# Hybrid S5 + mLSTM trunk on one core: S5 outputs by position, copies moved between engines, buffers and staging rearranged

## The chip, the cores and the metric

One Trainium2 chip, one core. The metric is the device time in microseconds of one execution. Its engines are TensorE (PE in the profile, its weight loads PEld), VectorE (DVE), ScalarE (ACT), GpSimd (POOL) and SyncE (SP, which issues the DMA transfers here).

## What is computed

One layer of a streaming encoder on x of 2048 positions x 1024 channels, then a final RMSNorm:

```python
h = rmsnorm(x, g);  p = h @ W_in
u, q_raw, k_raw, v, o_raw, i_raw, f_raw = split(p)
y_ssm = s5_mixer(u)     # 32 groups x 16 channels, one 64-dim complex state per group
                        # y = Re(C x) + D u ; z = gelu(y); z * sigmoid(z @ w_glu + b); rmsnorm
y_ml = mlstm_mixer(...) # 4 heads x 128; width-4 conv + SiLU on q, k; gates; rmsnorm per head
x = x + concat(y_ssm, y_ml) @ W_out
x = x + relu(rmsnorm(x) @ W1)^2 @ W2     # 1024 -> 4096 -> 1024
return rmsnorm(x)
```

## The kernel before

**Number format.** Large products run in fp16 as three matmuls: high x high, high x low, low x high (mm3, lines 155 to 161, where L159, L160 and L161 are the three). The high part is made by a scaled copy, the low part by a scaled subtraction. Weights are scaled and split when loaded (load_w, from L127): the usual path is one ACT copy with a scale (L140) and one DVE scalar_tensor_tensor (L141) per slice of 128 rows. With E=G it is, for eight slices, a DVE scaling of each (L134), an ACT copy for each two (L136) and a POOL subtraction for each two (L137). S5's small matmuls are in float32.

**Stages of the trace.** 0 to 150 us: input norm, the u projection, S5 tables. 150 to 690: the mixers, 16 blocks b (4 heads x 4 blocks of 512 positions). 690 to 740: the turn to the output projection. 740 to 912: output projection. 912 to 1500: FFN phase 0 (first half of the positions). 1500 to 2110: phase 1. To 2181: the last FFN outputs and the final norm.

**Mixer.** Block b makes q and k for the next block (proj_qk: 24 matmuls into a PSUM tile pq; then ACT copies pq to xc behind three halo columns, L236, and starts the convolution, L237; POOL copies the halo in, L239, and the next one out, L244; three DVE steps, L247; tanh; L250), v and the output gate (proj_vo), scores (mix_scores), the running state (mix_state) and the output (mix_out). mix_out multiplies the gate by the numerator, sums squares on ACT (L889), makes the norm factor in v4 with small DVE and POOL operations (L892 to L896) and scales og by v4 on POOL (L897). mix_store(b), called in block b+1, transposes og on PE (L904), splits it (L908, L909) and stores it to DRAM (L910).

**S5.** Sixteen units u of two groups run in blocks 0 to 10. s5_const(u) makes tables that depend on parameters only: inm and xt (POOL through helper line L603, DVE through L606), ge (three POOL copies, L630 to L632), the Toeplitz matrix in PSUM tile pgg (PE, L636 and L637, from ge and xt), its four shifted copies into m0 (ACT, L643) and the D term added to m0 by two DVE instructions (L645); then inT (L648, L650), the rotation table rh (POOL and DVE, one buffer) and four transfers from rh to rt (L670, on SP's queue; rt has two buffers). s5_state(u) transposes u (L686), projects it to states (L691), rotates (L694 to L698), scans (L700) and rotates back into sv (L702 to L708). s5_out(u) makes py: for each of two halves and two groups one matmul of m0 (L718) and one of xt (L719). Then GELU on ACT and DVE (L722 to L726) into uz. The GLU steps (glu_a, L764, reads uz by position within 8) follow from block 11 on. PSUM pool psa (tag "ax") has two buffers, shared by pgg, pit, put, pw and py.

**FFN.** A Strassen-like scheme with seven products. In a loop of phase 0, each step issues twelve matmuls of 512 columns (L1351 to L1353). The second operands, for phase 1, are made beside it by a generator hprep1 of 60 steps: loads of b, the norm (L1137), differences (L1146), a split on ACT and POOL (L1081, L1082), a store to DRAM. From loop step HP1 = 46 on, every second step advances it by one.

**Order.** Each engine takes its queue in order. The order is made by a planner at build time, which simulates a timeline and places each instruction when its simulated inputs are ready, so work of later units may stand far ahead of its place in the program. Tiles of one tag are handed out in program order.

**Memory.** Pools are stacked from two sides. The first two hop tiles (operands of the FFN products and before them of the output projection, pool hopa) lie on the right side behind r3, over addresses that the late mixer tiles used. The store of the last mixer block and the load of the first hop go through SP's queue (L910, L1292).

Of the kernel before, what the change touches and what calls it, by code (L numbers as in the profile page):

```python
# [9 lines left out]
F32 = mybir.dt.float32  # L10
# [7 lines left out]
P = 128  # L18
# [11 lines left out]
SLACK = 6  # L30
HP1 = 46
HB = 256
# [15 lines left out]
def trunk(  # L48
# [176 lines left out]
    def proj_qk(b, w):  # L225
# [12 lines left out]
        if t > 0:  # L238
            G.tensor_copy(xc[:, 0:3], halo[w])  # L239
        else:  # L240
            G.memset(xc[:, 0:3], 0.0)
        if t < NTB - 1:
            hl = smal.tile([P, 3], F32, name=f"hl{nm}{w}", tag=f"hl{w}", bufs=2)
            G.tensor_copy(hl, xc[:, TB:TB + 3])  # L244
            halo[w] = hl
# [32 lines left out]
    G.memset(Jm, 1.0)  # L278
    G.affine_select(out=Jm.rearrange("p (q i) -> p q i", i=8), in_=Jm.rearrange("p (q i) -> p q i", i=8), pattern=[[-1, 16], [16, 8]], compare_op=ALU.is_equal, fill=0.0, base=-112, channel_multiplier=1)
    pwr = cp.tile([P, 9, NG], F32, name="pwr")  # L280
# [314 lines left out]
    def s5_const(u):  # L595
# [20 lines left out]
        def bk(a, n):  # L616
            return a.unsqueeze(2).to_broadcast([P, 2, n, 16])
# [11 lines left out]
        gev = ge.rearrange("p g e (j q) -> p g e j q", q=16)  # L629
        G.tensor_copy(gev[:, :, 0, 0::2, :], bk(eb, 4))  # L630
        G.tensor_copy(gev[:, :, 0, 1::2, :], bk(inm[:, :, 1], 4))
        G.tensor_copy(gev[:, :, 1, 1::2, :], bk(eb, 4))  # L632
        pg = psa.tile([P, 2, P], F32, name=f"pgg{u}", tag="ax")
        for g in range(2):
            xf = xt[:, g].rearrange("p k q -> p (k q)")
            T.matmul(pg[:, g, 0:16], ge[:, g, 1, :], xf[:, 0:16], start=True, stop=True)  # L636
            T.matmul(pg[:, g, 16:128], ge[:, g, 0, :], xf[:, 0:112], start=True, stop=True)  # L637
        m0 = m02[u % 2]
        m0v = m0.rearrange("p g (q i) -> p g i q", i=8)
        pgv = pg.rearrange("p g (i q) -> p g i q", q=16)  # L640
        for a in range(4):
            o = 6 - 2 * a
            S.copy(m0v[32 * a:32 * a + 32, :, o:8, :], pgv[32 * a:32 * a + 32, :, 0:8 - o, :])  # L643
        for g in range(2):
            V.scalar_tensor_tensor(out=m0[:, g, :], in0=Jm, scalar=ct[:, O_D + g0 + g:O_D + g0 + g + 1], in1=m0[:, g, :], op0=ALU.mult, op1=ALU.add)  # L645
        pit = psa.tile([P, 2, P], F32, name=f"pit{u}", tag="ax")
# [4 lines left out]

        rh = st("rh", (2, 16, 16))
        tc_, td_ = (st(t, (2, 16, 16))[:, 0] for t in ("t1", "t2"))
# [57 lines left out]
    def s5_out(u):  # L711
        g0 = 2 * u
        xt, m0 = s5u.pop(u)[0:2]
        us, sv = s5s.pop(u)
        py = psa.tile([P, 2, 2, P], F32, name=f"py{u}", tag="ax")
        for h in range(2):
            for g in range(2):
                T.matmul(py[:, h, g, :], us[:, g, h, :], m0[:, g, :], start=True, stop=False)  # L718
                T.matmul(py[:, h, g, :], sv[:, g, h * P:(h + 1) * P], xt[:, g, 1:9, :].rearrange("p k q -> p q k"), start=False, stop=True)  # L719

        y2 = s5.tile([P, 2, 2, P], F32, name=f"y2{u}", tag="y2")
        S.activation(out=y2, in_=py, func=AF.Square)  # L722
        V.scalar_tensor_tensor(out=y2, in0=y2, scalar=1.0 / 0.044715, in1=py, op0=ALU.add, op1=ALU.mult)
        S.activation(out=y2, in_=y2, func=AF.Tanh, scale=GC * 0.044715)
        for h in range(2):
            V.scalar_tensor_tensor(out=uz[h][:, g0:g0 + 2, :], in0=y2[:, h], scalar=1.0, in1=py[:, h], op0=ALU.add, op1=ALU.mult)  # L726
        if u % 4 == 3:
            m = u // 4
            for h in range(2):
                V.tensor_reduce(out=zmx[:, h, m:m + 1], in_=uz[h][:, 8 * m:8 * m + 8, :].rearrange("p g n -> p (g n)"), axis=AX.X, op=ALU.max, apply_absolute_value=True)  # L730
# [28 lines left out]
    def glu_a(n):  # L759
# [3 lines left out]
        zc = gp.tile([P, 512], F32, name=f"zc{n}", tag="zc", bufs=3)  # L763
        V.tensor_scalar(out=zc.rearrange("p (g q) -> p g q", q=16), in0=uz[h].rearrange("p g (q i) -> p i g q", i=8)[:, i], scalar1=zs, scalar2=None, op0=ALU.mult)  # L764
        pz = psl.tile([P, 4, P], F32, name=f"pz{n}", tag="ml")
# [104 lines left out]
    def mix_out(b):  # L870
# [25 lines left out]
        V.scalar_tensor_tensor(out=v4, in0=v4, scalar=0.5, in1=rc, op0=ALU.mult, op1=ALU.mult)  # L896
        G.tensor_tensor(out=og, in0=og, in1=v4.unsqueeze(2).to_broadcast([P, 4, P]), op=ALU.mult)  # L897

# [16 lines left out]
    def load_wo(i, slot=0, wp=None, tag=None):  # L915
        wo[i], m = load_w(wout[i], KD, 256, O_GOUT, f"out{i}", slot, wp, tag, E=G)
        r_w[i] = descale(m, 2.0 ** -24, f"out{i}", tag="dsw")
# [62 lines left out]

    accxp = ctx.enter_context(pool("accx", side="right"))
    r3 = ctx.enter_context(pool("r3", side="right"))
    hopa = ctx.enter_context(pool("hopa", side="right"))
    hopp = [hopa, hopa] + [None] * 5
# [572 lines left out]
    for i in range(N + LAG):  # L1557
        if i < N:
            next(f1)
        if i >= HP1 and (i - HP1) % 2 == 0:  # L1560
            next(hp1, None)
# [96 lines left out]
```

## Time and profile before

| | |
|---|---|
| Median of 3 runs | 2182.2 us (2182.05 to 2182.97) |
| Profiled execution, own time | 2182.95 us |
| Its span | 2180.9 us |
| Mean granted TensorE clock | 0.982 |
| PE busy | 2042.0 us, 94% |
| DVE busy | 1711.0 us, 78% |
| ACT busy | 1062.5 us, 49% |
| POOL busy | 1150.6 us, 53% |

The profiled execution is one program run recorded by the hardware profiler. Busy time is the time in which an engine had an instruction running; shares are of the span. Matmuls overlap at their ends, so a busy PE is an upper reading of its work. "a <- b" after a group names what released it from its idle time: the instruction or transfer that came last. The chain of waits follows the work that ended last back through its releasers, and gives each line's share.

### The profile page before, as it was taken

To read this page: it belongs to the slowest core of one execution; us is meant where nothing else is said; L and a number is where in the kernel's file an instruction comes from. 1 tells how busy PE (TensorE), PEld (TensorE's weight loads), DVE (VectorE), ACT (ScalarE), POOL (GpSimd) and SP (SyncE) were. 2 spreads that over 40 slices of the span, in tenths; PEclk is the share of its full clock that TensorE was granted. 3 is DMA by queue.
4 is the path that set the end of the run, shared out by engine and by line. 5 is a ranking of instruction groups with operands and counts; after the bars stand their busy time and mean duration, and the time that the engine had idled before them with its cause. 6 is when DMAs were issued, how large, how long until landed. Compare 5 with 4: busy or idle time off the path is not lost.

```text
span 2180.9 us, 30020 instructions
## 1 busy us (share of the span) xinstructions
PE 2042.0 (94%) x11205; PEld 1162.8 (53%) x11205; DVE 1711.0 (78%) x2850; ACT 1062.5 (49%) x1902; POOL 1150.6 (53%) x1112
## 2 busy tenths in 40 slices
PE   6999998899999699999899999999999999999996
PEld 4986777677676344444344443444444444444445
DVE  7878888877867645769898999887888887677776
ACT  5425555555544322355454554555565555554543
POOL 2135656564323302466656766756685667565635
PEclk9999999999999899999999999999999999999998
DMA  4211111212103212311222222215342232111112
GB/s 167 68 52 54 54 40 35 73 35 64 59 20 115 108 39 77 112 49 44 92 87 69 101 92 77 79 53 199 99 153 97 97 116 81 55 67 50 39 39 78
DMA packets 55732, 168.18 MB, mean 77 GB/s; under 512 B 7905, under 2 KB 21409, under 8 KB 43041
## 3 DMA queue, kind: packets, MB, share of 16 engines
q1 hardware_dynamic: 55584, 166.26, 22.7%
q8 instruction: 88, 1.44, 0.3%
q14 instruction: 60, 0.48, 0.1%
HBM read 129.44 MB, written 28.41 MB: 72 GB/s over the span
## 4 chain that ended last, share of the span: by engine, by line
PE 48%; DVE 26%; POOL 7%; DMA 5%; issue 5%; ACT 4%; SPq 1%; POOLq 0%; DVEq 0%; ACTq 0%
DVE w2o L1227 3%; PE gx L1351 3%; PE gx L1352 3%; PE gx L1353 3%; PE fx L1351 3%; PE fx L1352 3%; PE fx L1353 3%; DMA r<-in_w_dram 3%; DVE x L1447 2%; PE po L159 2%; PE po L160 2%; PE po L161 2%; DVE y L247 2%; PE fv L1351 1%; PE fv L1352 1%
## 5 line engine op out<-in xcount | busy, mean ns | idle before, releaser
L1226 ACT ACTIVATE w2o<-r,fs_b 128x768 f16<-128x768 f32 (+1 forms) x128 | 105.4, 824 | 135.3 <-POOL r L1284 60.2
L1352 PEld LDWEIGHTS <-w2o 128*128 128x128 f16 x952 | 93.3, 98 | 131.8 <-issue 36.5
L1380 ACT ACTIVATE e<-e 128x512 f32<-128x512 f32 x96 | 60.3, 628 | 203.7 <-DVE e L1416 89.2
L1227 DVE SCALAR_TENSOR_TENSOR w2o<-r,fs_b,w2o 128x768 f16<-128x768 f32 (+1 forms) x128 | 134.7, 1053 | 25.1 <-ACT w2o L1226 24.3
L1353 PEld LDWEIGHTS <-w2o 128*128 128x128 f16 x952 | 93.1, 98 | 103.9 <-DVE w2o L1227 3.2
L1351 PEld LDWEIGHTS <-w2o 128*128 128x128 f16 x952 | 93.5, 98 | 103.0 <-ACT w2o L1226 3.1
L161 PE MATMUL pv<-w_vo,xn 128*128 128x256 f16 x512 | 141.1, 276 | 0.4 <-DVE xn L445 0.3
L159 PE MATMUL pv<-w_vo,xn 128*128 128x256 f16 x512 | 141.2, 276 | 0.0
L160 PE MATMUL pv<-w_vo,xn 128*128 128x256 f16 x512 | 141.2, 276 | 0.0
L1447 DVE SCALAR_TENSOR_TENSOR x2b<-gx,dd,x2b 128x512 f32<-128x512 f32 x112 | 82.7, 744 | 53.1 <-PE gx L1353 53.0
L1284 POOL TENSOR_TENSOR r<-r,s 128x256 f32<-128x256 f32 x64 | 63.9, 999 | 111.8 <-DVE w2o L1227 111.8
L1447 DVE SCALAR_TENSOR_TENSOR x<-gx,dd,x 128x512 f32<-128x512 f32 x128 | 94.2, 741 | 10.7 <-PE gx L1353 10.5
L1240 POOL TENSOR_TENSOR s<-r 128x512 f32<-128x512 f32 x32 | 54.1, 1690 | 85.4 <-issue 59.9
L159 PE MATMUL pq<-xn,w_qk 128*128 128x512 f16 x256 | 99.0, 387 | 0.0
L160 PE MATMUL pq<-xn,w_qk 128*128 128x512 f16 x256 | 98.7, 386 | 0.0
L161 PE MATMUL pq<-xn,w_qk 128*128 128x512 f16 x256 | 98.7, 385 | 0.0
L1351 PE MATMUL fx<-hop,wB 128*128 128x512 f16 x256 | 97.0, 379 | 0.7 <-ACT e L1409 0.7
L1352 PE MATMUL fx<-hop,wB 128*128 128x512 f16 x256 | 97.0, 379 | 0.0
L1353 PE MATMUL fx<-hop,wB 128*128 128x512 f16 x256 | 97.0, 379 | 0.0
L159 PEld LDWEIGHTS <-xn 128*128 128x128 f16 x768 | 87.8, 114 | 9.8 <-ACT xn L444 0.5
L160 PEld LDWEIGHTS <-xn 128*128 128x128 f16 x768 | 87.8, 114 | 9.4 <-issue 0.5
L161 PEld LDWEIGHTS <-xn 128*128 128x128 f16 x768 | 87.5, 114 | 8.9 <-DVE xn L445 1.8
(1326 smaller groups left out, 6940.0 us busy)
## 6 DMA issues: line engine op xcount, KB each, us to landing
r<-in_w_dram SPq DMA_DIRECT2D x64, 1024.0 KB, 4.9
xt<-in_xN_dram SPq DMA_DIRECT2D x16, 512.0 KB, 4.3
rt<-rh SPq DMA_DIRECT2D x64, 128.0 KB, 2.3
hopd<-ho SPq DMA_DIRECT2D x28, 256.0 KB, 2.6
hop<-hopd SPq DMA_DIRECT2D x7, 1024.0 KB, 4.7
st_vo<-in_wvo_dram SPq DMA_DIRECT2D x4, 1024.0 KB, 5.2
st_qk<-in_wqk_dram SPq DMA_DIRECT2D x4, 1024.0 KB, 5.2
bcm<-negM_d SPq DMA_DIRECT2D x16, 256.0 KB, 3.1
```

Source lines behind the costliest of these rows:

```text
L159: T.matmul(out, wh, xh, start=(i == 0), stop=False)
L160: T.matmul(out, wh, xl, start=False, stop=False)
L161: T.matmul(out, wl, xh, start=False, stop=(i == n - 1))
L1226: S.activation(out=hi, in_=src, func=AF.Copy, scale=sg)
L1227: V.scalar_tensor_tensor(out=lo, in0=src, scalar=sg, in1=hi, op0=ALU.mult, op1=ALU.subtract)
L1240: G.tensor_tensor(out=s12[:, 0], in0=raw[:, 2], in1=raw[:, 3], op=ALU.add)
L1284: G.tensor_tensor(out=r[:, 1], in0=r[:, 1], in1=s12[:, 1], op=ALU.subtract)
L1351: T.matmul(out, wh, xh, start=(first and i == 0), stop=False, skip_group_check=True)
L1352: T.matmul(out, wh, xl, start=False, stop=False, skip_group_check=True)
L1353: T.matmul(out, wl, xh, start=False, stop=(last and i == n - 1), skip_group_check=True)
L1380: S.activation(out=x, in_=x if src is None else src, func=AF.Relu, scale=scale)
L1447: V.scalar_tensor_tensor(out=acc[:, j, c, :], in0=bk[b], scalar=dd, in1=acc[:, j, c, :], op0=ALU.mult, op1=ALU.add)
```

## The change

In the S5 units the py columns go by position (i, then q) instead of (q, then i): m0, the D pattern Jm, the moving operand of L719 and the read in glu_a follow. The D term is added in PSUM, on the 32 columns where it lies, ahead of the four copies; a small table Jd is made for that at the start with four POOL copies. The ge copies, the halo copies and the og norm move from POOL to ACT (the norm as four activations with a scale per partition); the next halo is read from PSUM. rh has two buffers. load_wo takes load_w's usual path. Pool hopa is opened before r3. hprep1 starts at step 38 and is advanced in three of eight steps.

```diff
--- before.py
+++ after.py
@@ -28,7 +28,7 @@
 NFB = DFF // 256
 XF = 128.0
 SLACK = 6
-HP1 = 46
+HP1 = 38
 HB = 256
 NHD = 23
 EPS = 1e-6
@@ -236,12 +236,12 @@
         S.activation(out=xc[:, 3:], in_=pq, func=AF.Copy)
         S.activation(out=y, in_=pq, func=AF.Identity, scale=wc[:, 3:4], bias=cb[:, w:w + 1])
         if t > 0:
-            G.tensor_copy(xc[:, 0:3], halo[w])
+            S.copy(xc[:, 0:3], halo[w])
         else:
             G.memset(xc[:, 0:3], 0.0)
         if t < NTB - 1:
             hl = smal.tile([P, 3], F32, name=f"hl{nm}{w}", tag=f"hl{w}", bufs=2)
-            G.tensor_copy(hl, xc[:, TB:TB + 3])
+            S.copy(hl, pq[:, TB - 3:TB])
             halo[w] = hl
         for j in range(1, 4):
             V.scalar_tensor_tensor(out=y, in0=xc[:, 3 - j:3 - j + TB], scalar=wc[:, 3 - j:4 - j], in1=y, op0=ALU.mult, op1=ALU.add)
@@ -276,7 +276,11 @@
     G.memset(sgn[64:128], -1.0)
     Jm = cp.tile([P, P], F32, name="Jm")
     G.memset(Jm, 1.0)
-    G.affine_select(out=Jm.rearrange("p (q i) -> p q i", i=8), in_=Jm.rearrange("p (q i) -> p q i", i=8), pattern=[[-1, 16], [16, 8]], compare_op=ALU.is_equal, fill=0.0, base=-112, channel_multiplier=1)
+    G.affine_select(out=Jm.rearrange("p (i q) -> p i q", i=8), in_=Jm.rearrange("p (i q) -> p i q", i=8), pattern=[[16, 8], [-1, 16]], compare_op=ALU.is_equal, fill=0.0, base=-112, channel_multiplier=1)
+
+    Jd = cp.tile([P, 32], F32, name="Jd")
+    for a_ in range(4):
+        G.tensor_copy(Jd[32 * a_:32 * a_ + 32, :], Jm[32 * a_:32 * a_ + 32, (6 - 2 * a_) * 16:(8 - 2 * a_) * 16])
     pwr = cp.tile([P, 9, NG], F32, name="pwr")
     pwi = cp.tile([P, 9, NG], F32, name="pwi")
     Lc = cp.tile([P, 16, 16], F32, name="Lc")
@@ -627,29 +631,29 @@
 
         ge = ge2[u % 2]
         gev = ge.rearrange("p g e (j q) -> p g e j q", q=16)
-        G.tensor_copy(gev[:, :, 0, 0::2, :], bk(eb, 4))
-        G.tensor_copy(gev[:, :, 0, 1::2, :], bk(inm[:, :, 1], 4))
-        G.tensor_copy(gev[:, :, 1, 1::2, :], bk(eb, 4))
+        S.copy(gev[:, :, 0, 0::2, :], bk(eb, 4))
+        S.copy(gev[:, :, 0, 1::2, :], bk(inm[:, :, 1], 4))
+        S.copy(gev[:, :, 1, 1::2, :], bk(eb, 4))
         pg = psa.tile([P, 2, P], F32, name=f"pgg{u}", tag="ax")
         for g in range(2):
             xf = xt[:, g].rearrange("p k q -> p (k q)")
             T.matmul(pg[:, g, 0:16], ge[:, g, 1, :], xf[:, 0:16], start=True, stop=True)
             T.matmul(pg[:, g, 16:128], ge[:, g, 0, :], xf[:, 0:112], start=True, stop=True)
+        for g in range(2):
+            V.scalar_tensor_tensor(out=pg[:, g, 0:32], in0=Jd, scalar=ct[:, O_D + g0 + g:O_D + g0 + g + 1], in1=pg[:, g, 0:32], op0=ALU.mult, op1=ALU.add)
         m0 = m02[u % 2]
-        m0v = m0.rearrange("p g (q i) -> p g i q", i=8)
+        m0v = m0.rearrange("p g (i q) -> p g i q", i=8)
         pgv = pg.rearrange("p g (i q) -> p g i q", q=16)
         for a in range(4):
             o = 6 - 2 * a
             S.copy(m0v[32 * a:32 * a + 32, :, o:8, :], pgv[32 * a:32 * a + 32, :, 0:8 - o, :])
-        for g in range(2):
-            V.scalar_tensor_tensor(out=m0[:, g, :], in0=Jm, scalar=ct[:, O_D + g0 + g:O_D + g0 + g + 1], in1=m0[:, g, :], op0=ALU.mult, op1=ALU.add)
         pit = psa.tile([P, 2, P], F32, name=f"pit{u}", tag="ax")
         for g in range(2):
             T.transpose(pit[:, g, :], inm[:, g].rearrange("p k q -> p (k q)"), ident)
         inT = st("inT", (2, P))
         S.copy(inT, pit)
 
-        rh = st("rh", (2, 16, 16))
+        rh = st("rh", (2, 16, 16), 2)
         tc_, td_ = (st(t, (2, 16, 16))[:, 0] for t in ("t1", "t2"))
 
         def hk(a):
@@ -716,7 +720,7 @@
         for h in range(2):
             for g in range(2):
                 T.matmul(py[:, h, g, :], us[:, g, h, :], m0[:, g, :], start=True, stop=False)
-                T.matmul(py[:, h, g, :], sv[:, g, h * P:(h + 1) * P], xt[:, g, 1:9, :].rearrange("p k q -> p q k"), start=False, stop=True)
+                T.matmul(py[:, h, g, :], sv[:, g, h * P:(h + 1) * P], xt[:, g, 1:9, :].rearrange("p k q -> p (k q)"), start=False, stop=True)
 
         y2 = s5.tile([P, 2, 2, P], F32, name=f"y2{u}", tag="y2")
         S.activation(out=y2, in_=py, func=AF.Square)
@@ -761,7 +765,7 @@
         gp = gl["p"]
         zs = gl["z"][1][:, h:h + 1]
         zc = gp.tile([P, 512], F32, name=f"zc{n}", tag="zc", bufs=3)
-        V.tensor_scalar(out=zc.rearrange("p (g q) -> p g q", q=16), in0=uz[h].rearrange("p g (q i) -> p i g q", i=8)[:, i], scalar1=zs, scalar2=None, op0=ALU.mult)
+        V.tensor_scalar(out=zc.rearrange("p (g q) -> p g q", q=16), in0=uz[h].rearrange("p g (i q) -> p i g q", i=8)[:, i], scalar1=zs, scalar2=None, op0=ALU.mult)
         pz = psl.tile([P, 4, P], F32, name=f"pz{n}", tag="ml")
         for m in range(4):
             T.transpose(pz[:, m, :], zc[:, m * P:(m + 1) * P], ident)
@@ -894,7 +898,8 @@
         V.tensor_scalar(out=v4, in0=v4, scalar1=0.25 / P, scalar2=EPS, op0=ALU.mult, op1=ALU.add)
         G.tensor_tensor(out=v4, in0=v4, in1=nhalf, op=ALU.pow)
         V.scalar_tensor_tensor(out=v4, in0=v4, scalar=0.5, in1=rc, op0=ALU.mult, op1=ALU.mult)
-        G.tensor_tensor(out=og, in0=og, in1=v4.unsqueeze(2).to_broadcast([P, 4, P]), op=ALU.mult)
+        for c in range(4):
+            S.activation(out=og[:, c, :], in_=og[:, c, :], func=AF.Copy, scale=v4[:, c:c + 1])
 
     def mix_store(b):
         h, t = b // NTB, b % NTB
@@ -913,7 +918,7 @@
     wo, r_w = [None] * 4, [None] * 4
 
     def load_wo(i, slot=0, wp=None, tag=None):
-        wo[i], m = load_w(wout[i], KD, 256, O_GOUT, f"out{i}", slot, wp, tag, E=G)
+        wo[i], m = load_w(wout[i], KD, 256, O_GOUT, f"out{i}", slot, wp, tag)
         r_w[i] = descale(m, 2.0 ** -24, f"out{i}", tag="dsw")
 
     mix_load(0)
@@ -979,8 +984,8 @@
 
 
     accxp = ctx.enter_context(pool("accx", side="right"))
+    hopa = ctx.enter_context(pool("hopa", side="right"))
     r3 = ctx.enter_context(pool("r3", side="right"))
-    hopa = ctx.enter_context(pool("hopa", side="right"))
     hopp = [hopa, hopa] + [None] * 5
     accx = [None] * 4
 
@@ -1557,7 +1562,7 @@
     for i in range(N + LAG):
         if i < N:
             next(f1)
-        if i >= HP1 and (i - HP1) % 2 == 0:
+        if i >= HP1 and (i - HP1) * 3 % 8 < 3:
             next(hp1, None)
         if i == 16:
             w2_scale(0, 0)
```

## Rows read from the trace of the kernel before

**Rows 1.** Windows: us, busy us (instructions) of PE, PEld, DVE, ACT, POOL; clock, DMA.

```profile
150.00:565.00 415.00, 385.11 (x2658) 299.45 (x2657) 336.19 (x663) 219.78 (x535) 233.75 (x292) 0.97 0.18 50
...
690.00:740.00 50.00, 26.15 (x157) 17.35 (x155) 36.28 (x88) 16.86 (x39) 17.71 (x16) 0.83 0.53 195
...
1000.00:1415.00 415.00, 389.43 (x1785) 176.60 (x1784) 374.02 (x511) 208.40 (x310) 275.45 (x228) 0.99 0.24 81
1415.00:1500.00 85.00, 84.99 (x398) 39.05 (x396) 69.17 (x102) 45.31 (x65) 47.60 (x43) 1.00 0.25 92
```

**Rows 2.** Chain of waits, 150 to 565 us: its sum by line.

```profile
by line: DVE y L247 8.9%; DMA rt<-rh 4.9%; DVE t L700 4.8%; issue 4.3%; ACT m L643 3.6%; SPq L670 3.2%; PE pq L159 2.9%; PE pq L160 2.8%; DVE w_vo L141 2.7%; PE pq L161 2.6%; DVE t L698 2.3%; DVE m L645 2.3%; DVE rh L606 2.0%; DVE t L704 1.
```

**Rows 3.** Groups of PE by shape, 150 to 565 us: busy us, mean ns, idle before.

```profile
L719 PE MATMUL py<-xt,sv 128*128 128x128 f32 x128 | 38.6, 391 | 6.1 <-POOL sv L708 4.7 <-POOL xc L241 1.3
L718 PE MATMUL py<-m,us 128*128 128x128 f32 x128 | 26.3, 287 | 1.7 <-ACT m L643 1.7
...
L904 PE MATMUL pT<-ident,og 128*128 128x128 f32 x44 | 7.1, 284 | 6.7 <-POOL og L897 5.0 <-POOL sv L707 1.7
```

**Rows 4.** Timeline of PE at 452 us: start us, us, engine, line.

```profile
452.49 0.39 PE L718 MATMUL py<-m,us 128*128 128x128 f32 x2
452.71 0.60 PE L719 MATMUL py<-xt,sv 128*128 128x128 f32 x2
453.13 0.40 PE L718 MATMUL py<-m,us 128*128 128x128 f32 x2
```

**Rows 5.** Groups of DVE by shape, 150 to 565 us.

```profile
L645 DVE SCALAR_TENSOR_TENSOR m<-Jm,ct,m 128x128 f32<-128x128 f32 x32 | 16.7, 561 | 7.3 <-ACT m L643 7.3
...
L865 DVE SCALAR_TENSOR_TENSOR C<-C,gbc,pst 128x129 f32<-128x129 f32 x39 | 13.4, 342 | 8.5 <-PE pst L860 8.3
...
L606 DVE TENSOR_TENSOR rh<-Hs,Lc 128x256 f32<-128x256 f32 x15 | 12.3, 822 | 14.6 <-DMA rt<-rh 14.6
...
L885 DVE TENSOR_TENSOR rc<-pn,gcol 128x2 f32<-128x2 f32 x22 | 3.3, 149 | 0.2 <-PE pn L883 0.2
```

**Rows 6.** Line 645 alone: duration ns minimum/median/maximum.

```profile
L645 DVE SCALAR_TENSOR_TENSOR m<-Jm,ct,m x32: 321/350/1357, 164.6 to 524.4; 128x128 f32<-128x128 f32 x32
```

**Rows 7.** Groups of POOL by shape, 150 to 565 us.

```profile
L603 POOL TENSOR_TENSOR rh<-Hc,Lc 128x256 f32<-128x256 f32 x15 | 16.5, 1098 | 22.1 <-DMA rt<-rh 20.3 <-DVE og L887 1.7
...
L897 POOL TENSOR_TENSOR og<-og,v 128x512 f32<-128x512 f32 x11 | 14.2, 1289 | 4.8 <-DVE v L896 4.7
...
L632 POOL COPY ge<-bcA 128x128 f32<-128x128 f32 x15 | 7.7, 515 | 34.1 <-PE pgg L636 34.1
```

**Rows 8.** Window 150 to 565 us, instructions on tile ge alone.

```profile
150.00:565.00 415.00, 18.60 (x128) 17.57 (x128) 21.32 (x45) 0.97 0.18 50
```

**Rows 9.** Groups of ACT by shape, 150 to 565 us.

```profile
L829 ACT ACTIVATE sc<-bcm,gbc 128x128 f32<-128x128 f32 x44 | 14.2, 389 | 0.1
...
L889 ACT ACTIVATE kw<-og 128x128 f32<-128x128 f32 x44 | 13.1, 300 | 6.9 <-DVE og L887 6.8
...
L643 ACT COPY m<-pgg 32x256 f32<-32x256 f32 x16 | 9.9, 620 | 0.2
...
L650 ACT COPY inT<-pit 128x256 f32<-128x256 f32 x16 | 5.9, 369 | 1.0 <-PE pit L648 0.7
```

**Rows 10.** Timeline of PE, 709 to 733 us.

```profile
731.41 0.77 PE L98 MATMUL pmx_out<-ident,m_out 128*128 128x128 f32 x2 [13.52 <-DVE m_out L110]
```

**Rows 11.** Timeline of SP's issues, 716 to 733 us.

```profile
722.05 0.33 SPq L910 DMA_DIRECT2D ml_d<-mo  x1
722.47 0.38 SPq L129 DMA_DIRECT2D st_out<-in_wout_dram  x1
```

**Rows 12.** Timeline of POOL, 715 to 733 us.

```profile
716.92 2.45 POOL L137 TENSOR_TENSOR w_out<-st_out,w_out 128x512 f16<-128x512 f32 x2
```

**Rows 13.** Groups of DVE by shape, 1000 to 1415 us.

```profile
L1137 DVE SCALAR_TENSOR_TENSOR b<-b,ct,rsh 128x512 f32<-128x512 f32 x16 | 19.0, 1200 | 0.0
...
L1146 DVE TENSOR_TENSOR b<-b,b 128x512 f32<-128x512 f32 x12 | 15.5, 1291 | 3.2 <-POOL ho L1082 3.2
```

## Prediction, made before the result was known

> **What bounds the kernel now.** I read the page first, then a table by stage. In the mixer, 150 to 565 us, PE is busy 385.11 of 415.00 us, DVE 336.19 (81%), POOL 233.75 (56%) and ACT 219.78 (53%) [rows 1]: PE comes close to full, so the stage is worth attacking in two ways only, fewer PE microseconds or fewer PE stalls. The idle 29.9 us is the least that stalls cost here, as ends of matmuls are modelled. The other stages that the change touches are the turn from mixer to FFN (690 to 740, PE 26.15 of 50) and FFN phase 0 (1000 to 1415, PE 389.43 of 415, DVE 374.02); from 1415 to 1500 PE is full at 84.99 of 85 with DVE at 69.17 [rows 1].
>
> Then the chain of waits for the mixer: it is not on one engine. DVE y L247 has 8.9%, the transfer rt<-rh 4.9% and SP's issue of it (L670) 3.2%, the m copies (L643, ACT) 3.6%, the D term (L645, DVE) 2.3% [rows 2]. So an S5 unit's table, Toeplitz block and scan run beside the projections, and PE stalls where the planner's order expects them sooner than they come. Last, the groups by engine and the PE timeline, for the durations below.
>
> **Outputs by position (L719).** The second matmul of a py pair reads xt with q before k, a stride of 16 elements; it takes 391 ns, where L718 with the same shape takes 287 [rows 3]. In the timeline a pair is 452.49, 452.71, 453.13: the strided one holds PE 0.42 us, the other 0.22 [rows 4]. The new order reads xt contiguously. If L719 falls to 0.22 to 0.24 us, a pair gains 0.19, and 16 units x 4 pairs x 0.19 = **12 us**, all of it PE time and PE is the fullest engine. Were the stride not the reason (L718 differs from it in weights only), it is 0. I take 12: same shape, type and engine, and the moving operand's order is what differs. The other end stays in the range.
>
> The same layout makes the target of the four m copies contiguous. The largest takes 620 ns for 32x256, the inT copy 369 for 128x256 from the same kind of PSUM tile, contiguous on both sides [rows 9]: 16 x 0.25 = 4 us of ACT for this size alone, in a chain of which L643 holds 3.6% [rows 2]. The zc read in the GLU gets runs of 16 in place of a stride; I cost it at nothing, since at worst it stays as it is.
>
> **D term in PSUM (L645).** Removed: 32 x 561 ns = 18 us (16.7 us in the window [rows 5]) on SBUF 128x128. Added: 32 instructions of 128x32 with one PSUM input. No such row exists. The nearest from PSUM are L865, 128x129 at 342 ns, and L885, 128x2 at 149 [rows 5]: in proportion 149 + 30/127 x 193 = 195 ns, so 32 x 0.195 = 6.2 and DVE loses 10 to 11 us. With L885 as one end and L865 as the other the new term is 4.8 to 10.9 us. In a stage where DVE is 81% busy and PE 93% little of that is path: 2.3% of 415 us is 9.5 us of chain [rows 2], of which a part goes and the next chain takes over. I take **2**, between 0 and 6.
>
> The old row's minimum is 321 ns, its median 350 and its maximum 1357 [rows 6]. So the mean of 561 comes from some instructions that were held up, and the unhindered saving is only 0.35 - 0.20 = 0.15 us each, 5 us in all. [...]
>
> **Copies and norm off GpSimd.** POOL loses the ge copies (21.32 us, x45 [rows 8]), the og norm (11 x 1289 ns = 14.2 us) [rows 7] and the 3-column halo copies. ACT gains 48 ge copies at some 0.30 (L889, 128x128, 300 ns), 4 scaled copies per block at 0.389 (L829 with a pointer, 44 here = 17.1 us), and 32 halo copies of at most 0.30 each [rows 9]: 14.4 + 17.1 + 9.6 = 41, less 4 = **37 us**, so ACT goes from 53% to 62%. POOL falls by over 35 us, to 48%. What is bought: PE waited 5.0 us for og at L904 and 4.7 us for POOL's sv at L719 [rows 3]. The norm's latency falls little (four times 0.389 = 1.56 against 1.29 us), but it need no longer queue behind POOL's 1.3 to 1.6 us tables. I take 60% of these 9.7 us, **6** (sv's own tables stay on POOL), and charge ACT's fuller queue **2** (py and pT wait for its evacuations): net 4. Bounds: 10 gained to 34 lost (last rival).
>
> **Two table buffers (rh).** DVE stood 14.6 us [rows 5] and POOL 20.3 us [rows 7] before the next rh, waiting for the transfer out of the only one. With two, unit u+1's table no longer waits for unit u's transfer. But the order of each queue is made by a planner which places an instruction as soon as its simulated inputs are there; with two buffers it will place the table one unit earlier, and the same late transfer holds it then. The rt tiles, which L670 fills, had two buffers and have two. I take **0**, to 20 gained.
>
> **Projection inputs placed lower, load_wo.** The later load_wo calls drop eight DVE scalings, four ACT copies and four POOL subtractions for eight ACT scalings (L140's form) and eight DVE instructions (L141's form). That balance is near zero. In the transition PE stands 13.52 us, until 731.41, for m_out [rows 10], which waits for the last load_wo's load, issued by SP at 722.47, right behind the store of mo at 722.05 [rows 11]. The staging tile was free when POOL's last two subtractions ended, 716.92 + 2.45 = 719.37 [rows 12]. So POOL's part can bring at most 3.1 us as long as the store stands first in SP's queue, and it is the store that decides: it needs og, whose norm now leaves POOL for ACT. The first hop input moves to addresses not shared with the late mixer tiles, so it may be loaded sooner; but it still reads what this store writes. I take **3**, from 0 to 13.5.
>
> **Second operands spread.** Three steps in eight instead of one in two: 60 steps over 160 loop steps in place of 120. In 1000 to 1415 PE makes 1785 matmuls [rows 1], 12 to a loop step, so 149 steps of 2.79 us. PE falls 25.6 us short there, DVE is 90% busy. The side stream's largest DVE groups are L1137 (16 x 1200) and L1146 (12 x 1291) [rows 13], 34.5 us; spreading takes a quarter of it, 9 us, out of the thickest stretch into 1415 to 1500, where DVE has 16 us free. But all the DVE work stays, and the base alone is (374-34.5)/415 = 82%. **5**, from 0 to 15.
>
> **The sum.** 12 + 2 + 4 + 0 + 3 + 5 = 26. The profiled execution took 2182.95 us (span 2180.9), 0.75 above the median of 2182.2 of the three runs: 2182.95 - 26 = 2157, and against the median **2156 us**, 1.2% less.
>
> **Rivals.** (1) The waits really go: rh's second buffer lets tables run ahead, and of the 14.6 + 20.3 = 34.9 us that DVE and POOL stood for it [rows 5, 7] 15 come off the path, giving 2141; all of it gives 2156 - 35 = 2121, with the held-up L645 rows running without POOL's company besides. For it: the 321-to-1357 spread. Against it: the planner. [...]
> (2) The savings are off the path: only the PE time of L719 counts, other stalls refill; 2170.
> (3) Nothing: stride is not what costs L719, and PE's waits are replaced by others; 2182.
> (4) Slower: ACT inherits POOL's queue. Before L632, POOL stood 34.1 us for PE's pgg (the ge tile's last reader) [rows 7]. On POOL that hurt little, at 56%. In front of ACT's in-order queue the same wait stands ahead of projection evacuations that PE needs for its PSUM buffers. If all of it lands on PE, -26 + 34 = +8, 2190. It decides once ACT's idle time ahead of the ge copies is over 26 us and PE's stalls name ACT.
>
> **Chances.** Forecast (2145 to 2165) 0.42; rival 1 0.22; rival 2 0.20; rival 3 0.06; rival 4 0.10. A difference under 0.2%, 4.4 us, can't be told from none. Rivals 2 and 3 both give some of the middle: 0.16 faster and 0.04 same, and 0.06 same. Faster: 0.42 + 0.22 + 0.16 = 0.80; same 0.10; slower 0.10. The range, 2121 to 2184, leaves out rival 4 and what of rival 1 overlaps with larger gains elsewhere.
>
> **What would show it.** Right: L719 near 287 ns, and 0.22 us between starts; L645 near 0.2 us with a narrow spread; ACT near 62% and POOL under 50% in the mixer; waits of rh on rt still there; PE's 13.5 us hole a little shorter; DVE under 90% in 1000 to 1415. Wrong: L719 unchanged, ACT waiting on pgg, stalls of PE on ACT, or a hole in the transition that closes altogether.

## The result and the profile after

Median 2169.6 us (four runs, 2163.7 to 2171.0) against 2182.1 before: ratio 0.9937, 95% interval 0.9918 to 0.9956, so 12.5 us or 0.6% faster. The forecast was 2156. The time lies inside the stated range and is faster as expected, by about half of what the sum said. The profiled execution is the fastest of the four, 2163.7 us (span 2161.7), 19.2 under the profiled one of before; the slower three had a granted clock of 0.975 to 0.977 against its 0.982.

The windows of the changed kernel (columns as in [rows 1]):

```profile
150.00:565.00 415.00, 380.38 (x2706) 297.30 (x2705) 335.35 (x669) 239.24 (x660) 192.99 (x204) 0.97 0.18 51
...
690.00:740.00 50.00, 34.82 (x181) 20.58 (x179) 34.37 (x89) 20.71 (x53) 6.92 (x8) 0.86 0.58 213
...
1000.00:1415.00 415.00, 394.18 (x1823) 179.62 (x1821) 371.19 (x525) 210.10 (x311) 267.08 (x221) 1.00 0.23 78
1415.00:1500.00 85.00, 84.86 (x397) 38.98 (x395) 71.28 (x86) 47.00 (x70) 61.96 (x54) 1.00 0.45 160
```

POOL went from 56% to 47% of the mixer window, near the 48 of the forecast. ACT went from 53% to 58% and not to 62: it gained 19.5 us where 37 were forecast. In the turn to the output projection PE has 34.8 us busy instead of 26.2. In 1000 to 1415 PE gained 4.8 us, where DVE went from 374.0 to 371.2.

Windows of fixed ends mix work, so from here on the stages are cut by the work itself: at the start of the last u projection matmul (pu), the last py, the last pn, the last pmx_out, the first FFN matmul and the 2401st FFN matmul on record, each in its own trace; "rest" runs to the start of the last FFN matmul. (py makes the S5 outputs, pn the mLSTM numerators; pmx_out is the last step of PE ahead of the output projection.) Times in us:

| kernel (profiled execution) | mixer: pu to py | py to pn | turn: pn to pmx_out | projection | phase 0 | rest |
|---|---|---|---|---|---|---|
| before | 397.4 | 148.3 | 24.5 | 204.1 | 563.8 | 661.3 |
| changed | 391.2 | 148.5 | 18.1 | 204.0 | 555.4 | 661.9 |
| changed, second set | 392.3 | 149.9 | 18.3 | 204.5 | 555.5 | 662.1 |
| layout only | 392.7 | 148.9 | 23.6 | 204.8 | 564.0 | 661.3 |
| og norm on POOL | 385.4 | 148.1 | 19.3 | 204.8 | 556.3 | 661.4 |
| ge copies on POOL | 378.0 | 148.8 | 18.3 | 207.4 | 555.8 | 662.2 |
| both on POOL | 384.5 | 149.2 | 19.4 | 204.7 | 555.7 | 661.7 |
| second operands as before | 391.2 | 148.6 | 18.3 | 207.3 | 563.4 | 662.0 |
| hopa after r3 | 391.8 | 148.5 | 18.1 | 204.2 | 555.6 | 662.1 |
| load_wo's old path | 391.8 | 150.0 | 19.2 | 204.6 | 555.4 | 661.6 |
| one rh buffer | 389.8 | 148.8 | 18.5 | 205.5 | 556.6 | 661.7 |
| ge copies on POOL, D term in SBUF | 386.9 | 146.8 | 18.2 | 204.0 | 556.0 | 661.4 |
| og norm on POOL, store later | 385.7 | 142.6 | 21.5 | 204.5 | 556.3 | 661.6 |
| inT first, turn's POOL work back | 380.6 | 147.3 | 21.5 | 205.3 | 556.0 | 661.2 |

The 19.2 us of the profiled execution are 6.2 in the mixer, 6.4 in the turn and 8.4 in phase 0, with 1.2 us lost ahead of the mixer and about 0.6 elsewhere. The mixer was forecast at 18 (12 + 2 + 4).

The groups that answer to [rows 3], PE in 150 to 565 us (L723 is the old L719, L722 the old L718, L909 the old L904):

```profile
L723 PE MATMUL py<-xt,sv 128*128 128x128 f32 x128 | 25.9, 285 | 2.1 <-POOL sv L712 1.9
L722 PE MATMUL py<-m,us 128*128 128x128 f32 x128 | 25.3, 280 | 1.5 <-ACT m L649 0.8 <-ACT inT L654 0.7
...
L909 PE MATMUL pT<-ident,og 128*128 128x128 f32 x44 | 13.4, 323 | 18.5 <-ACT og L902 18.5
```

L723 is now as fast as L722. But the transposes of og wait 18.5 us for the norm, now L902 on ACT; they waited 6.7 before. DVE and POOL, answering to [rows 5] and [rows 7] (L643 is the D term in PSUM, L610 and L607 the helper lines of old L606 and L603):

```profile
L610 DVE TENSOR_TENSOR rh<-Hs,Lc 128x256 f32<-128x256 f32 x14 | 10.8, 768 | 8.9 <-DMA rt<-rh 8.7 <-issue 0.2
...
L643 DVE SCALAR_TENSOR_TENSOR pgg<-Jd,ct,pgg 128x32 f32<-128x32 f32 x32 | 7.8, 244 | 8.7 <-PE pgg L641 8.5
```

```profile
L607 POOL TENSOR_TENSOR rh<-Hc,Lc 128x256 f32<-128x256 f32 x14 | 17.2, 1229 | 25.3 <-DMA rt<-rh 25.3
```

The D term takes 244 ns against the 195 worked out, and its spread (line alone, minimum/median/maximum) is gone:

```profile
L643 DVE SCALAR_TENSOR_TENSOR pgg<-Jd,ct,pgg x32: 217/245/256, 163.9 to 513.8; 128x32 f32<-128x32 f32 x32
```

The waits before rh on the transfer are still there: 8.7 us on DVE, 25.3 on POOL. ACT, answering to [rows 9]:

```profile
L902 ACT ACTIVATE og<-og,v 128x128 f32<-128x128 f32 x44 | 14.2, 391 | 14.8 <-DVE v L900 14.7
...
L649 ACT COPY m<-pgg 32x256 f32<-32x256 f32 x16 | 5.8, 366 | 0.2
...
L635 ACT COPY ge<-inm 128x128 f32<-128x128 f32 x16 | 4.7, 294 | 4.2 <-POOL inm L607 4.0
...
L636 ACT COPY ge<-bcA 128x128 f32<-128x128 f32 x14 | 4.1, 294 | 7.7 <-PE pgg L640 7.6
```

The largest m copy fell from 620 to 366 ns, as the contiguous target let expect; all four sizes together went from 28.3 to 18.0 us, where the forecast counted 4 us for the largest alone. But ACT now stands idle ahead of the norm (14.8 us, for the factor v) and ahead of the ge copies (4.2 + 7.7). The chain of waits, answering to [rows 2], names neither: it still begins with the convolution and keeps the transfer rt<-rh, while the m copies and the D term have left its head.

```profile
by line: DVE y L247 8.9%; DVE t L704 4.7%; DMA rt<-rh 4.3%; issue 4.1%; SPq L674 3.2%; DVE t L708 2.8%; DVE ta L610 2.8%; PE pq L159 2.5%; DVE t L702 2.5%; DVE rh L610 2.4%; PE pq L160 2.4%; PE pq L161 2.3%; DVE y L250 2.1%; DVE w_vo L141 2
```

In the turn, PE's hole is 8.47 us instead of 13.52 [rows 10], and SP issues the last weight load ahead of the store of mo, not behind it [rows 11]; the first hop load went out 18.7 us before that store:

```profile
720.20 0.77 PE L98 MATMUL pmx_out<-ident,m_out 128*128 128x128 f32 x2 [8.47 <-DVE m_out L110]
```

```profile
694.77 0.50 SPq L1297 DMA_DIRECT2D hop0ml<-ml_d  x1
...
711.96 0.33 SPq L129 DMA_DIRECT2D st_out<-in_wout_dram  x1
713.42 0.32 SPq L915 DMA_DIRECT2D ml_d<-mo  x1
```

### The profile page after: what moved, and what is told of

Same layout as the page of the kernel before. It is cut to its first block, busy times and chain, and to the rows that moved or that the text cites. A ratio compares the mean times of both kernels' runs of the same rounds, so it can differ in the third digit from the quotient of the medians.

```text
span 2161.7 us, 30038 instructions
## 1 busy us (share of the span) xinstructions
PE 2030.1 (94%) x11205; PEld 1157.4 (54%) x11205; DVE 1694.4 (78%) x2850; ACT 1090.4 (50%) x2078; POOL 1082.9 (50%) x988
## 4 chain that ended last, share of the span: by engine, by line
PE 52%; DVE 28%; POOL 6%; DMA 5%; ACT 4%; issue 4%; SPq 1%; POOLq 0%; DVEq 0%; ACTq 0%
DVE w2o L1232 3%; DMA r<-in_w_dram 3%; PE gx L1356 3%; PE gx L1358 3%; PE gx L1357 3%; PE fx L1357 3%; PE fx L1356 3%; PE fx L1358 3%; DVE x L1452 3%; PE po L159 2%; PE po L161 2%; PE po L160 2%; DVE y L247 2%; PE gv L1358 1%; PE gv L1356 1%
## 5 line engine op out<-in xcount | busy, mean ns | idle before, releaser
L1231 ACT ACTIVATE w2o<-r,fs_b 128x768 f16<-128x768 f32 (+1 forms) x128 | 105.2, 824 | 148.5 <-POOL r L1289 70.5
```

Source lines behind the costliest of these rows:

```text
L1231: S.activation(out=hi, in_=src, func=AF.Copy, scale=sg)
```

## The experiments

All ratios are to the kernel before in the same set of runs. "Changed" is 0.9937 in its first set and 0.9922 (0.9910 to 0.9935) in the second. Each kernel below is the changed one with the edit shown, unless said otherwise.

**The changed kernel again.** No edit.

> The changed kernel once more, unchanged. Its four runs lay between 2163.7 and 2171.0 us where the kernel before keeps within 1.1. If two orders of arrival of some transfer decide, the runs fall into two groups near 2164 and 2170, and the profile of a slower one is late from one place on; if it is a slow drift, they fill the space between.

Five runs, 2166.4 to 2168.7, median 2167.65, granted clocks 0.976 to 0.978. Taken with the first four, 2163.7 to 2171.0, the times fill the space between and go roughly with the clock (2163.7 at 0.982, 2166.4 at 0.978, 2171.0 at 0.975, but also 2168.7 at 0.978). The kernel before spreads too when it is run more often: 2181.0 to 2185.6 us in the eleven runs of this set. The stages (table) are the same but for 1.1 us in the mixer and 1.4 behind it.

**Layout by position alone**, put into the kernel before (Jm's pattern and the GLU's read of uz change with it and are not shown):

```diff
-m0v = m0.rearrange("p g (q i) -> p g i q", i=8)
+m0v = m0.rearrange("p g (i q) -> p g i q", i=8)
-... xt[:, g, 1:9, :].rearrange("p k q -> p q k") ...
+... xt[:, g, 1:9, :].rearrange("p k q -> p (k q)") ...
```

> The kernel before with the layout by position alone (D term still added in SBUF, all copies on POOL, one table buffer). Theory: the stride was what L719 cost; L719 falls from 391 to about 285 ns, and the time by 8 to 14 us, to 2168 to 2174. Rival: PE's saved time turns into waits; L719 falls but the time stays within 4 us of before.

2179.0 us, ratio 0.9975 (0.9965 to 0.9986): 5.1 us less than before, between the two expectations. The windows of the same stage, pu to py, in the kernel before and in this one:

```profile
161.30:558.90 397.60, 367.71 (x2499) 282.70 (x2498) 328.55 (x645) 214.43 (x522) 227.35 (x284) 0.97 0.17 49
```

```profile
160.90:553.80 392.90, 355.53 (x2499) 271.11 (x2498) 328.77 (x645) 203.49 (x517) 229.62 (x284) 0.97 0.18 49
```

The same 2499 matmuls take 355.5 us of PE instead of 367.7: the 12.2 us of the stride came in full. PE's idle time rose from 29.9 to 37.4 us: 7.5 of the 12.2 were given back as waits. DVE's busy time did not change (328.55, 328.77); PE reached its waits sooner.

**The og norm back on POOL:**

```diff
-for c in range(4):
-    S.activation(out=og[:, c, :], in_=og[:, c, :], func=AF.Copy, scale=v4[:, c:c + 1])
+G.tensor_tensor(out=og, in0=og, in1=v4.unsqueeze(2).to_broadcast([P, 4, P]), op=ALU.mult)
```

> The changed kernel with the og norm back on POOL (one instruction). Theory: the 12 us of L719 came in full, and the mixer shows only 5 because PE's transposes pT now wait some 21 us for the og norm on ACT instead of 6 for POOL; then this runs 8 to 14 us faster than the changed kernel, 2150 to 2160, and the pT stall falls to under 8 us. Rival: pT's wait is only where PE's slack shows, the norm factor being late on any engine; then the time stays within 4 us of the changed kernel and the stall moves to another matmul of the mixer.

2162.3 us, ratio 0.9900 (0.9887 to 0.9914): 5.3 us less than the changed kernel's second set, short of the 8 to 14. And the reason given falls: the transposes (PE's groups, 150 to 565 us) wait as long as in the changed kernel.

```profile
L908 PE MATMUL pT<-ident,og 128*128 128x128 f32 x44 | 8.4, 322 | 21.1 <-POOL og L901 17.5 <-POOL sv L711 3.6
```

21.1 us, of which 17.5 for og on POOL. So the norm is late on either engine, and the wait at pT is not the price of ACT. From the og product on DVE to the end of the norm the first eleven mixer blocks take 6 to 17 us each in these traces (8 to 15 in the kernel before, 9 to 11 in the changed one): squares, four small DVE operations that stand between long ones, the power on POOL and the scaling. The stretch did not become longer in the changed kernel; PE comes to the transposes sooner.

**Second operands as before:**

```diff
-HP1 = 38
+HP1 = 46
-if i >= HP1 and (i - HP1) * 3 % 8 < 3:
+if i >= HP1 and (i - HP1) % 2 == 0:
```

> The changed kernel with the second operands made as before, from step 46 on and every second step. Theory: the 8 us that phase 0 gained (the FFN's 2400th matmul is 19.7 us earlier where the first was 11.3) come from the spread; then this is 6 to 10 us slower than the changed kernel. Rival: they come from the shifted start of phase 0 and the loads' new timing; then it is within 3 us.

2172.3 us, ratio 0.9948 (0.9934 to 0.9961), 4.6 over the changed kernel by the medians, between the two expectations. Phase 0 takes 563.4 us in its trace against 555.5: 7.9, nearly all of the gain of 8.4, so that by the stage the first expectation holds. Its windows over the stretches of [rows 1]:

```profile
1000.00:1415.00 415.00, 387.07 (x1785) 175.59 (x1784) 374.45 (x510) 209.55 (x312) 271.45 (x224) 1.00 0.24 82
1415.00:1500.00 85.00, 85.00 (x397) 38.88 (x396) 66.55 (x98) 45.00 (x65) 50.30 (x44) 1.00 0.31 108
```

DVE is at 374.45 as before, PE at 387.07 against 394.18 in the changed kernel; from 1415 on DVE has 66.55 instead of 71.28. That is the shift that was forecast: 3 to 5 us of DVE work moved behind 1415 give PE 7.

**The ge copies back on POOL:**

```diff
-S.copy(gev[:, :, 0, 0::2, :], bk(eb, 4))
+G.tensor_copy(gev[:, :, 0, 0::2, :], bk(eb, 4))
...
```

> The changed kernel with the three ge copies back on POOL. With the og norm on POOL the mixer's last pn was 11.7 us earlier than before, with the layout alone 4.4: some 7 us come from the other mixer parts. Theory: freeing POOL of the ge copies is most of that; then this is 3 to 8 us slower than the changed kernel (2167.7 and 2169.6 in two sets of runs). Rival: on ACT they delay its queue as the og norm does, in front of PE's transposes; then it is 2 to 5 us faster. A third: neither, within 2 us, since POOL has idle time and ACT too.

2154.4 us, ratio 0.9865 (0.9850 to 0.9880): 13 us faster than the changed kernel, the fastest of the study. The theory had it slower, the rival 2 to 5 us faster. The mixer stage in the changed kernel and in this one:

```profile
162.40:553.80 391.40, 357.35 (x2499) 275.66 (x2498) 321.47 (x644) 229.50 (x631) 188.16 (x199) 0.97 0.18 49
```

```profile
164.00:542.20 378.20, 348.98 (x2499) 267.52 (x2497) 319.48 (x644) 217.37 (x588) 202.69 (x242) 0.99 0.18 51
```

Of 13.2 us PE's idle time is 4.8 (34.05 to 29.22) and the time of the same 2499 matmuls 8.4 (357.35 to 348.98), at a granted clock of 0.99 instead of 0.97. POOL takes the wait that ACT had, and longer (its groups, 150 to 565 us):

```profile
L636 POOL COPY ge<-bcA 128x128 f32<-128x128 f32 x16 | 4.9, 309 | 40.7 <-PE pgg L640 40.7
```

40.7 us of idle time ahead of L636 there, as 34.1 before [rows 7], against 7.6 + 0.6 + 4.0 = 12.2 ahead of the three copies on ACT. But ACT's idle time is no measure of what the move cost: ahead of the norm ACT stands longer here than in the changed kernel (25.2 against 14.8 us), while PE's wait for og falls from 18.5 to 10.0 (groups of ACT and of PE, 150 to 565 us):

```profile
L902 ACT ACTIVATE og<-og,v 128x128 f32<-128x128 f32 x44 | 14.1, 391 | 25.2 <-DVE v L900 25.2
```

```profile
L909 PE MATMUL pT<-ident,og 128*128 128x128 f32 x44 | 12.2, 290 | 10.0 <-ACT og L902 10.0
```

**Both back on POOL**, the two edits above together.

> The changed kernel with both the ge copies and the og norm back on POOL. The ge copies alone gave 13 us back (2154.4), the og norm alone 5 (2162.3). Theory: they are two separate head-of-line waits on ACT (12.2 us of ACT idle ahead of ge, 14.7 ahead of og in the changed kernel), and the gains add: 2146 to 2152. Rival: both act through one thing, PE reaching pT too early, and the second undo brings little or takes some back: 2153 to 2162.

2163.4 us, ratio 0.9911 (0.9894 to 0.9927). The gains do not add: the second undo takes 9 us back, and the time lies just over the rival's range. Its mixer stage:

```profile
162.80:547.50 384.70, 351.52 (x2500) 270.26 (x2499) 323.06 (x644) 206.83 (x548) 217.48 (x252) 0.98 0.18 50
```

PE's idle time is 33.2 us. So neither move has a price of its own that could be read off one undo.

**One rh buffer:**

```diff
-rh = st("rh", (2, 16, 16), 2)
+rh = st("rh", (2, 16, 16))
```

> The changed kernel with one rh buffer. Theory as predicted: the planner moves the table a unit ahead and it waits for the same transfer, so the time stays within 2 us of the changed kernel. Rival: the second buffer brought part of the 7 us in the mixer; then it is 3 to 8 us slower, with more idle time of DVE and POOL before rh than the 8.7 and 25.3 us of the changed kernel.

2165.7 us, ratio 0.9923 (0.9906 to 0.9939), that of the changed kernel. The waits before rh, on DVE and on POOL, are somewhat longer than with two (11.3 and 29.9 against 8.7 and 25.3) and cost nothing:

```profile
L610 DVE TENSOR_TENSOR rh<-Hs,Lc 128x256 f32<-128x256 f32 x14 | 10.8, 768 | 11.5 <-DMA rt<-rh 11.3 <-issue 0.2
```

```profile
L607 POOL TENSOR_TENSOR rh<-Hc,Lc 128x256 f32<-128x256 f32 x14 | 17.5, 1248 | 29.9 <-DMA rt<-rh 29.9
```

**hopa opened after r3:**

```diff
-hopa = ctx.enter_context(pool("hopa", side="right"))
 r3 = ctx.enter_context(pool("r3", side="right"))
+hopa = ctx.enter_context(pool("hopa", side="right"))
```

> The changed kernel with hopa opened after r3, as before. In the changed kernel the first hop load goes out at 695 us, 19 us ahead of the last store. Theory: the addresses held it back; here it is issued after the last mixer tiles are free, past 711, and lands 5 to 6 us later, about when m_out is ready (720) or a little past it: 0 to 5 us slower, and the load of st_out may queue behind it. Rival: the whole 6 us that the turn to the output projection gained come from it, by the SP queue; then it is 5 to 8 us slower.

2166.0 us, ratio 0.9922 (0.9907 to 0.9937): no difference, and the turn takes 18.1 us as in the changed kernel. The hop load now goes out behind the store, at 722.21, but the weight load stays ahead of it:

```profile
714.60 0.34 SPq L129 DMA_DIRECT2D st_out<-in_wout_dram  x1
...
716.06 0.67 SPq L915 DMA_DIRECT2D ml_d<-mo  x1
722.21 0.33 SPq L1297 DMA_DIRECT2D hop0ml<-ml_d  x1
```

**load_wo on its old path:**

```diff
-load_w(wout[i], KD, 256, O_GOUT, f"out{i}", slot, wp, tag)
+load_w(wout[i], KD, 256, O_GOUT, f"out{i}", slot, wp, tag, E=G)
```

> The changed kernel with load_wo on its old path (DVE scaling, ACT copy, POOL subtraction). The turn to the output projection is 5 to 6 us shorter in the changed kernel, and the place of hopa had no part in it. Theory: the staging tile is free at 711.9 instead of some 7 us later in the stage, so the last weight load is issued ahead of the store of mo; with the old path it goes back behind it, and the time is 4 to 8 us over the changed kernel's 2165 to 2170, at 2170 to 2177. Rival: the og norm on ACT or the planner's new order did it; then within 2 us of the changed kernel.

2163.9 us, ratio 0.9917 (0.9900 to 0.9933): no slower than the changed kernel; the expectation missed. The turn takes 19.2 us, 1.1 more.

**The D term back in SBUF**, with the ge copies on POOL (compare with 2154.4):

```diff
-V.scalar_tensor_tensor(out=pg[:, g, 0:32], in0=Jd, scalar=..., in1=pg[:, g, 0:32], ...)
+V.scalar_tensor_tensor(out=m0[:, g, :], in0=Jm, scalar=..., in1=m0[:, g, :], ...)
```

> The changed kernel with the ge copies back on POOL, and the D term added in SBUF after the copies, as before (on the new layout). Theory, as predicted: the D term in PSUM brings 0 to 6 us, so this is at 2154 to 2160. Rival: with the ge copies on POOL the mixer gains 16 us by the last pn, the layout alone 4.4, and most of the rest comes from the shorter path of the Toeplitz block: then 8 to 12 us slower than 2154.4, 2162 to 2166.

2159.2 us, ratio 0.9890 (0.9875 to 0.9905): 4.9 us slower by the medians, inside the 0 to 6. By the stages of the two traces the mixer alone is 8.9 us longer (386.9 against 378.0), which is the rival's size; 3.4 us come back in the projection and 2.0 between py and pn, where the kernel without this undo is the slower one. The D term (L646 here) has its wide spread again:

```profile
L646 DVE SCALAR_TENSOR_TENSOR m<-Jm,ct,m x32: 314/352/1358, 166.3 to 516.5; 128x128 f32<-128x128 f32 x32
```

**The store later**, with the og norm on POOL (compare with 2162.3):

```diff
-if b >= 1:
-    mix_store(b - 1)
 mix_scores(b)
...
 if us_ and us_[0] > 0:
     s5_out(us_[0] - 1)
+if b >= 1:
+    mix_store(b - 1)
```

> The changed kernel with the og norm on POOL, and with mix_store of the last block called after the first half of proj_vo and s5_out, in place of ahead of mix_scores. Theory: PE's 22 us of stalls before pT are the norm factor's latency on DVE's queue (the small operations stand behind 0.7 to 2 us ones), and PE loses it because pT stands too early in its order; later in the program it is placed later: the stall halves, and the time is 4 to 12 us under that of the og norm on POOL (2162.3), 2150 to 2158. Rival: the planner places pT by its simulated readiness whatever the program's order; then within 3 us of 2162. Slower is possible where the PSUM ring of pT is held longer.

2159.4 us, ratio 0.9894 (0.9874 to 0.9913): within 3 us of 2162.3, as the rival says for the time. But pT's stall did fall, from 21.1 to 6.5 us, and another rose in its place, at the transposes of k. By the stages, 5.5 us go between py and pn, and 2.2 come back in the turn, which takes 21.5 us.

```profile
L842 PE MATMUL pK<-ident,y 128*128 128x128 f32 x48 | 8.7, 298 | 9.7 <-DVE y L250 5.8 <-DVE ma_qk L115 3.9
L908 PE MATMUL pT<-ident,og 128*128 128x128 f32 x44 | 7.6, 289 | 6.5 <-POOL og L901 5.8 <-POOL sv L711 0.7
```

**Order alone, and the turn.** inT's block ahead of the ge copies in the program; load_wo's old path and the last block's norm on POOL:

```diff
+pit = psa.tile([P, 2, P], F32, name=f"pit{u}", tag="ax")
+...
+S.copy(inT, pit)
 ge = ge2[u % 2]
...
-pit = psa.tile([P, 2, P], F32, name=f"pit{u}", tag="ax")
-...
```

> Two separate questions, in two stages of one kernel, read by stage. Mixer (last u projection matmul to last py; the same 2499 matmuls in all kernels: 391.4 us in the changed kernel, 378.2 with the ge copies on POOL, 385.5 with the og norm on POOL, 384.7 with both): here inT's transposes and copy stand ahead of the ge copies in the program, same instructions, same engines. Theory: the moves off POOL act much through the order that the planner makes; then this reordering alone moves the stage by 4 to 12 us, either way. Rival: the engine loads decide; then it stays within 2 us of 391.4. Turn to the output projection (last pn to last pmx_out: 24.5 us before, 23.5 with the layout alone, 18.1 in the changed kernel, 19.1 with load_wo's old path, 18.1 with hopa's old place, 19.3 with the og norm on POOL): here load_wo's old path and the last block's og norm on POOL together. Theory: either one off POOL is enough, so that both back on POOL give 22 to 25 us, with the load of st_out issued behind the store of mo. Rival: 18 to 20 us, the load ahead of the store as in the changed kernel.

2157.2 us, ratio 0.9881 (0.9864 to 0.9898). The mixer takes 380.6 us instead of 391.2, with the same instructions on the same engines:

```profile
162.60:543.50 380.90, 352.43 (x2500) 270.44 (x2499) 311.38 (x644) 227.52 (x631) 183.04 (x199) 0.98 0.18 51
```

ACT is busy 227.5 us and POOL 183.0, as in the changed kernel (229.5 and 188.2). The order of the program alone, and with it the order in which pit and pgg take the two PSUM buffers, moved this stage by 10.6 us, almost as much as the ge copies' engine: PE's idle time falls from 34.05 to 28.47 us and the time of the same matmuls from 357.35 to 352.43. DVE, with the same 644 instructions, is busy 10.1 us less (311.38 against 321.47). In the turn, 21.5 us: half of the gain is gone. The load is still ahead of the store, which the theory had otherwise; but the staging tile is free only when POOL's last subtractions end (700.89 + 2.71 = 703.60), behind the norm:

```profile
703.63 0.33 SPq L129 DMA_DIRECT2D st_out<-in_wout_dram  x1
704.64 0.32 SPq L918 DMA_DIRECT2D ml_d<-mo  x1
```

```profile
699.66 1.27 POOL L902 TENSOR_TENSOR og<-og,v 128x512 f32<-128x512 f32 x1 [0.30 <-DVE v L900]
700.89 2.71 POOL L137 TENSOR_TENSOR w_out<-st_out,w_out 128x512 f16<-128x512 f32 x2
```

## Why the prediction was right in sign and half in size

**Outputs by position** (12 forecast): the price was exact, 12.2 us of PE for the same matmuls. What failed is the sentence "all of it PE time and PE is the fullest engine", from which the whole of it was put on the path. The layout alone gave 4.7 us of its stage; 7.5 became idle time. No rival had it so: rival 2 counted L719's 12 us in full and struck out the rest, rival 3 held that L719 would not change.

**D term** (2, between 0 and 6): 244 ns each, where 195 was worked out; 4.9 us by one undo. The range held by the medians, though the mixer stage says 8.9, and after the last experiment an effect of this size can also be order. The spread went from 321 to 1357 ns [rows 6] to 217 to 256. That the old rows were held up in POOL's company shows in the trace of the kernel before alone: there 18 of the 32 L645 took 321 to 352 ns, and each of the other 14 (444 to 1357) ended 147 to 151 ns after the end of a POOL instruction that ran beside it. Below, the second of two L645 ends at 431.96, POOL's product at 431.80. In the changed kernel 13 of the 32 L643 started while a POOL tensor_tensor was running, and they took 217 to 256 ns like the rest; why the term is not held up there, no run shows.

```profile
429.84 2.12 DVE L645 SCALAR_TENSOR_TENSOR m<-Jm,ct,m 128x128 f32<-128x128 f32 x2 [1.13 <-ACT m L643]
430.48 1.32 POOL L708 TENSOR_TENSOR sv<-t,t 128x512 f32<-128x512 f32 x1
```

**Copies and norm off POOL** (net 4 gained): this is the step that failed. It bought 60% of the waits that POOL's users had, 5.0 us for og and 4.7 for sv, because the norm "need no longer queue behind POOL's 1.3 to 1.6 us tables". The wait for sv did fall, to 1.9 us; the wait for og rose to 18.5 us on ACT and stayed at 17.5 with the norm back on POOL, so which of the two engines scales og did not decide it. ACT's load was oversized (37 us forecast, 19.5 measured) and did not decide. Undoing the ge copies gave 13 us back, undoing the norm 5, undoing both only 4. Two of the signs of being wrong showed: ACT waited on pgg, and PE's longest stall named ACT. The last rival had that place and direction and put 34 us on it; ACT's idle time ahead of the ge copies was 12.2 us, 8.2 of it for pgg, under the rival's deciding 26. That this wait is what cost the 13 us is argued and not shown.

**Table buffers** (0): right, and for the reason given: the waits stayed and moved with the planner.

**Turn** (3, up to 13.5): 6.4 us. The step "it still reads what this store writes" was wrong: the first hop load went out 18.7 us ahead of the last store, so what had held it was the address (with hopa in its old place it goes out at 722.21 instead of 694.77). It did not matter: with hopa in its old place the turn is as short. What the shorter turns looked at have in common (the changed kernel, the norm or the ge copies on POOL, hopa's old place, load_wo's old path) is the weight load ahead of the store on SP's queue, but the last kernel has that too and gives 3.4 us of the 6.4 back, and the kernel with the later store, its load also ahead, 3.4 as well. How much is SP's order and how much the staging tile's release is not settled.

**Second operands** (5, up to 15): 7.9 us by the undo's phase 0 and 4.6 by the medians, by the mechanism named; 3 to 5 us of DVE work moved, where 9 were worked out.

**The sum.** Mixer 18 forecast, 6.2 measured: PE is busy 10.4 us less for the same matmuls (357.35 instead of 367.71), and 4.2 of them came back as idle time (34.05 instead of 29.89); turn 3 and 6.4; phase 0 5 and 8.4; some 1.8 us lost ahead of the mixer and elsewhere that no term had. And the median lies 5.9 us above the profiled execution, where before it lay 0.75 under it. That the total came out at half is in part luck: the turn and phase 0 brought 6.8 us more than their terms, over half of the 11.8 that the mixer lacked. The median lies outside the forecast's own 2145 to 2165 and beside rival 2's 2170, but not by that rival's account, since the turn and phase 0 did gain and L719's 12 us did not count in full.

**What stays open.** Whether the ge copies' 13 us are the wait in ACT's queue or the order that came with them. The last run shows that order alone is worth as much, and the runs with both copies back on POOL don't fit a fixed price; no experiment here held the order still while moving the copies. Measured by those 10.6 us, the 4.7 us of the layout, the 5 of the norm and the 4.9 of the D term are no prices either.

## What to carry to other kernels

Time taken off the fullest engine was not worth its full price here, as the next waits were close behind (7.5 of 12.2 us came back as waits): compare that engine's idle time for the same work before and after, not its busy time alone. Before moving an instruction to a less busy engine, look at what it waits for: a copy whose wait of 34 us was harmless on POOL stood in front of other work on ACT, and the kernel was 13 us faster without that move, though not by a price that held in other surroundings. And where a planner lays out the order, run one reordering that changes no work, and read a single undo only beyond what that moves the time.

## What was not expected of the hardware

The same 2499 matmuls took PE 349.0 us at a granted clock of 0.99 and 357.4 at 0.97. In the changed kernel PE works through 371 to 374.9 at full clock, then stands 3.98 us for og; behind that the mean clock of the records is 0.56 (378.9 to 381.5 us). The windows, and PE's timeline around the hole:

```profile
371.00:374.90 3.90, 3.90 (x36) 3.48 (x34) 3.90 (x17) 2.48 (x9) 1.67 (x3) 1.00 0.06 15
378.90:381.50 2.60, 2.56 (x13) 2.57 (x14) 2.56 (x6) 2.06 (x6) 2.60 (x1) 0.56 0.27 38
```

```profile
374.57 0.27 PE L161 MATMUL pv<-w_vo,xn 128*128 128x256 f16 x1
374.68 0.27 PE L159 MATMUL pv<-w_vo,xn 128*128 128x256 f16 x1
378.94 0.33 PE L909 MATMUL pT<-ident,og 128*128 128x128 f32 x1 [3.98 <-ACT og L902]
...
379.39 0.42 PE L909 MATMUL pT<-ident,og 128*128 128x128 f32 x1
```

At full clock the same transposes take 0.27 us (at 455 to 457 us the granted clock is 1.00):

```profile
455.83 0.27 PE L909 MATMUL pT<-ident,og 128*128 128x128 f32 x1
```

So this stall was paid for a second time, in slower matmuls behind it (0.42 us for a transpose). Executions of one and the same kernel differ the same way: 2163.7 us at a granted clock of 0.982, 2171.0 at 0.975.
